# Values of stick-breaking attention by seven block products instead of eight

## The chip, the cores and the metric

The kernel runs on one core of a Trainium2 chip. The metric is the device time of one execution in microseconds (us), as the median of several runs. The engines that matter are TensorE (PE in the profile, with its weight loads as PEld), VectorE (DVE), ScalarE (ACT), GpSimd (POOL) and the queues of transfers that SyncE (SP) and GpSimd issue.

## The reference, cut to what matters

A trunk of two layers over 512 rows of 1024 columns, all in fp32. The first layer is gated linear attention and an MLP, the second stick-breaking attention and an MLP. What the change touches is this:

```python
h = layer_norm(ALPHA * h + mix, ...)                # mix: gated attention, ends with o @ w_o
h = layer_norm(ALPHA * h + sq_relu_mlp(h, w_up, w_down), ...)
kv = h @ kv_w                                       # 1024 x 2048
k_sh, v_sh = kv[..., :D], kv[..., D:]               # keys, values
q = h @ sb_w_q
# ... attention by blocks of 128 queries, then @ sb_w_o, layer_norm,
# and a second MLP with its layer_norm, whose result is the output
```

`sq_relu_mlp` is `relu(x @ w_up) ** 2 @ w_down`, with 4096 columns in between.

## The kernel before, in words

Every fp32 product is made of three matmuls. A number is split into `hi`, its rounding to the matrix engine's format fp32r, and `lo`, what is left; a product is hi by hi, hi by lo and lo by hi. For a tile of weights `split_tile` does it (L67): ScalarE copies to `hi` (L70), VectorE subtracts to `lo` (L72). For activations `put` does it (L97 to L99), out of PSUM or SBUF; tiles of split activations are named `T`. Weights come in tiles of 128 by 1024: `raw` for plain ones, with three buffers, and `B` for blocks that are added up. `hi` and `lo` have six buffers each.

The 512 rows are four row tiles, `hs[0]` to `hs[3]` (h300 to h303 in the profile's names). A row tile's work after a stage is: `add` (L163) of the two halves of 512 columns out of PSUM, statistics (L175 and L179 on VectorE, then `rs` on GpSimd, L184), `centre` (L188), `affine` by gain and bias (L194), and a turn: `turn_affine` (L219) transposes four 128 by 128 pieces on TensorE (L224), applies gain and bias to the columns on ScalarE (L227) and splits the result with `put`. So gain and bias are applied twice, once to the turned copy that the next product reads and once to the row tile that the residual needs. `finish` (L238) runs that for a stage's tiles and hands back the turns that it leaves to the next stage (`late`).

Two kinds of products exist. `rows` and its like multiply one row tile or column tile directly. `seven` (L274) multiplies a 512 by 1024 matrix by a 1024 by 1024 one as two by two blocks with seven block products in place of eight, after Strassen and Winograd. It needs sums and differences of blocks on both sides. A block product has 24 matmuls of 512 columns, two halves of 12 (`part`, L328). Sums of weights are made on VectorE, or, for the last call of a stage (`ends`), by accumulating transfers on GpSimd's queue (`more`, L286). `plain_b` (L312) is the one factor that is a plain block of weights. The kernel before uses `seven` for the output projection of gated attention and for the MLPs' way down. Each caller has a pool of its own for the blocks `B`.

The values (L741 to L747) are made by `rows`: for each half of 512 columns and each row tile 24 matmuls, 192 in all. The turns of row tiles 2 and 3 are done between them. ScalarE copies each result to SBUF (L745). Keys and queries of the first pair of heads follow.

In an MLP's last two groups of columns on the way up, ScalarE does both the relu and the square (L685 and L689); in the others VectorE multiplies (L687). At the very end `done1` gathers the statistics of each row tile, those of tiles 0 and 1 on ScalarE (`stats_apart`, L196), and `norm` (L208) applies mean, gain and bias on VectorE and stores.

A scheduler sets the order on each engine from the program's order and its own costs; an instruction that is wrapped in `keep_in_program_order` stays behind those that the program has ahead of it. Each engine runs its instructions in that order and waits on semaphores.

## Time and profile before

| | |
|---|---|
| median of 3 runs | 1141.9 us (1141.05 to 1141.96) |
| the profiled execution | 1141.15 us, its span 1139.4 us |
| TensorE busy | 1119.6 us (98%) |
| VectorE busy | 802.8 us (70%) |
| ScalarE busy | 559.3 us (49%) |
| GpSimd busy | 180.3 us (16%) |

A row of a timeline gives a start, a length, the engine, the line, and in square brackets the idle time before it with the engine, tile and line that ended it. A row of a group gives the count, the busy time, the mean length of one in ns, and the idle time before its instructions. Matmuls overlap, so a matmul's length is not its pace.

### The profile page before, as it was taken

To read this page: it belongs to the slowest core of one execution; us is meant where nothing else is said; L and a number is where in the kernel's file an instruction comes from. 1 tells how busy PE (TensorE), PEld (TensorE's weight loads), DVE (VectorE), ACT (ScalarE), POOL (GpSimd) and SP (SyncE) were. 2 spreads that over 40 slices of the span, in tenths; PEclk is the share of its full clock that TensorE was granted. 3 is DMA by queue.
4 is the path that set the end of the run, shared out by engine and by line. 5 is a ranking of instruction groups with operands and counts; after the bars stand their busy time and mean duration, and the time that the engine had idled before them with its cause. 6 is when DMAs were issued, how large, how long until landed. Compare 5 with 4: busy or idle time off the path is not lost.

```text
span 1139.4 us, 14091 instructions
## 1 busy us (share of the span) xinstructions
PE 1119.6 (98%) x5389; PEld 924.7 (81%) x5389; DVE 802.8 (70%) x972; ACT 559.3 (49%) x831; POOL 180.3 (16%) x225
## 2 busy tenths in 40 slices
PE   8999999999999999999999999999999999999996
PEld 7778887898888888887888877777988888888874
DVE  4576638977756846848946878787777767567478
ACT  4354436653533524636635666754545435336262
POOL 1010123020000100122302444340100000001221
PEclk9999999999999999999999999999999999999999
DMA  7441299493670770796344121211865816707871
GB/s 239 124 120 48 75 269 202 133 300 112 164 224 19 194 203 29 199 207 130 111 112 130 56 74 38 74 38 37 257 187 125 237 45 161 227 19 191 181 128 74
DMA packets 104936, 156.47 MB, mean 137 GB/s; under 512 B 12258, under 2 KB 37218, under 8 KB 104868
## 3 DMA queue, kind: packets, MB, share of 16 engines
q1 hardware_dynamic: 86916, 120.96, 33.1%
q0 software_dynamic: 17952, 34.61, 17.9%
q8 instruction: 42, 0.69, 0.2%
q14 instruction: 26, 0.21, 0.1%
HBM read 153.45 MB, written 2.10 MB: 137 GB/s over the span
## 4 chain that ended last, share of the span: by engine, by line
PE 80%; DVE 13%; ACT 3%; issue 2%; POOL 1%; DMA 0%; POOLq 0%; SPq 0%; DVEq 0%; ACTq 0%
PE ps L334 27%; PE ps L93 17%; PE ps L94 16%; PE ps L95 16%; DVE r L798 4%; DVE lo L72 3%; ACT wt L813 1%; DVE h L194 1%; DVE T L99 1%; DVE ps L790 1%; DVE h L168 1%; ACT hi L70 1%; DVE qs L773 1%; DVE bst L175 1%; POOL rs L184 1%
## 5 line engine op out<-in xcount | busy, mean ns | idle before, releaser
L334 PE MATMUL ps<-hi,T 128*128 128x512 f32 x1008 | 314.1, 390 | 3.7 <-ACT T L98 2.3
L93 PE MATMUL ps<-T,hi 128*128 128x512 f32 (+1 forms) x768 | 288.6, 376 | 0.0
L94 PE MATMUL ps<-T,hi 128*128 128x512 f32 (+1 forms) x768 | 285.8, 372 | 0.5 <-DVE T L99 0.4
L95 PE MATMUL ps<-T,lo 128*128 128x512 f32 (+1 forms) x768 | 285.4, 372 | 0.0
L72 DVE TENSOR_TENSOR lo<-raw,hi 128x1024 fp32r<-128x1024 f32 x134 | 163.8, 1226 | 136.5 <-ACT hi L70 136.1
L70 ACT ACTIVATE hi<-raw 128x1024 fp32r<-128x1024 f32 x134 | 142.7, 1068 | 198.7 <-PE ps L94 67.6
L334 PEld LDWEIGHTS ps<-hi,T 128*128 128x128 f32 x1008 | 189.1, 188 | 44.9 <-ACT T L98 4.1
L72 DVE TENSOR_TENSOR lo<-B,hi 128x1024 fp32r<-128x1024 f32 x108 | 131.1, 1223 | 93.3 <-ACT hi L70 93.1
L334 PE MATMUL ps<-lo,T 128*128 128x512 f32 x504 | 196.3, 389 | 0.0
L70 ACT ACTIVATE hi<-B 128x1024 fp32r<-128x1024 f32 x108 | 114.2, 1060 | 150.2 <-PE ps L94 103.6
L95 PEld LDWEIGHTS ps<-T,lo 128*128 128x128 f32 x768 | 144.7, 188 | 25.1
L94 PEld LDWEIGHTS ps<-T,hi 128*128 128x128 f32 x768 | 144.8, 189 | 24.6 <-DVE T L99 0.9
L93 PEld LDWEIGHTS ps<-T,hi 128*128 128x128 f32 x768 | 144.6, 188 | 24.5 <-issue 1.1
L288 POOL DMA_DIRECT2D B<-in_mlp_w_down_dram x52 | 62.5, 1231 | 539.8 <-DMA B<-in_mlp_w_down_dram 427.4
L334 PEld LDWEIGHTS ps<-lo,T 128*128 128x128 f32 x504 | 94.6, 188 | 19.4
L93 PE MATMUL ps<-hi,T 128*128 128x512 f32 x256 | 102.8, 402 | 0.0
L94 PE MATMUL ps<-lo,T 128*128 128x512 f32 x256 | 100.5, 393 | 0.0
L95 PE MATMUL ps<-hi,T 128*128 128x512 f32 x256 | 100.5, 393 | 0.0
L168 DVE TENSOR_TENSOR h<-h,ps 128x512 f32<-128x512 f32 x110 | 74.7, 681 | 7.0 <-PE ps L95 3.5
L798 DVE TENSOR_TENSOR_SCAN r<-r,begin 128x512 f32<-128x512 f32 x40 | 66.3, 1664 | 0.2
L799 POOL TENSOR_TENSOR w<-w,r 128x512 f32<-128x512 f32 x40 | 51.5, 1288 | 75.7 <-DVE r L798 60.4
L93 PEld LDWEIGHTS ps<-hi,T 128*128 128x128 f32 x256 | 48.6, 190 | 10.5 <-issue 1.3
(171 smaller groups left out, 1189.3 us busy)
## 6 DMA issues: line engine op xcount, KB each, us to landing
raw<-in_mlp_w_up_dram SPq DMA_DIRECT2D x64, 512.0 KB, 5.5
B<-in_mlp_w_down_dram SPq DMA_DIRECT2D x64, 512.0 KB, 4.9
B<-in_mlp_w_down_dram POOLq DMA_DIRECT2D x52, 512.0 KB, 7.9
raw<-in_gla_w_in_dram SPq DMA_DIRECT2D x20, 512.0 KB, 3.7
raw<-in_mlp_w_down_dram SPq DMA_DIRECT2D x16, 512.0 KB, 5.1
raw<-in_kv_w_dram SPq DMA_DIRECT2D x16, 512.0 KB, 3.8
B<-in_gla_w_o_dram POOLq DMA_DIRECT2D x14, 512.0 KB, 8.1
B<-in_gla_w_o_dram SPq DMA_DIRECT2D x8, 512.0 KB, 7.3
```

The costliest lines, as they stand in the source:

```text
L70: nc.scalar.activation(hi, raw, AF.Copy)
L72: nc.vector.tensor_tensor(lo, raw, hi.bitcast(F32), op=ALU.subtract)
L93: nc.tensor.matmul(ps, lhsT=a[0], rhs=b[0], start=first, stop=False)
L94: nc.tensor.matmul(ps, lhsT=a[0], rhs=b[1], start=False, stop=False)
L95: nc.tensor.matmul(ps, lhsT=a[1], rhs=b[0], start=False, stop=last)
L99: keep(nc.vector.tensor_tensor(lo, ps, hi.bitcast(F32), op=ALU.subtract))
L168: nc.vector.tensor_tensor(h, h, ps, op=op)
L175: nc.vector.bn_stats(out=self.st[:, n, :], in_=h)
L288: nc.gpsimd.dma_start(out=b.rearrange("p (a b) -> p a b", a=2), in_=weights(k, h, j), accum_op=ALU.add)
L334: nc.tensor.matmul(banks[s], lhsT=a(k, s)[x], rhs=b[k][y], start=opens and (k, x, y) == (0, 0, 0), stop=closes and (k, x, y) == (3, 1, 0), ...
L798: nc.vector.tensor_tensor_scan(down, down, begins[kind][:, ::-1], 1.0, op0=ALU.mult, op1=ALU.max)
L799: nc.gpsimd.tensor_tensor(w, w, r[:, 1:S + 1], op=ALU.mult)
```

## The change

Values are now made by `seven` too, 7 x 24 = 168 matmuls. The left factor is h as turned columns. Three of the seven products read blocks that are split already (q11, q12 and q22 of `h2T`). The others need sums of unsplit blocks of h; so an unsplit copy `hF` is kept: for row tiles 0 and 1 it is rebuilt as hi + lo, for tiles 2 and 3 the turn writes it. `Values.add` has ScalarE copy the first part of each result and VectorE add the rest.

The blocks `B` live in one pool from the output projection of gated attention to the values, and in a second one for the last MLP. In `plain_b` ScalarE's `hi` of plain weights keeps its place in the program, which is behind the splits of activations. In the MLPs' last two groups on the way up two of four squares go to VectorE. In the last stage the norms of row tiles 0 and 1 come with a later step, and a norm's first operation keeps its place.

```diff
@@ split_piece / split_tile
-        return split_tile(raw, a)
+        return split_tile(raw, a, **how)
...
+    def split_tile(raw, a, keep=lambda ins: ins):
...
-        nc.scalar.activation(hi, raw, AF.Copy)
+        keep(nc.scalar.activation(hi, raw, AF.Copy))
@@ norm
-                nc.vector.scalar_tensor_tensor(h, h, self.less, g, op0=ALU.add, op1=ALU.mult)
+                first = nc.vector.scalar_tensor_tensor(h, h, self.less, g, op0=ALU.add, op1=ALU.mult)
...
+            tc.keep_in_program_order(first)
@@ seven
-    def seven(a1, a2, weights, pool, hs, fresh, norms=(), mid=None, ends=False):
+    def seven(a1, a2, weights, pool, hs, fresh, norms=(), mid=None, ends=False,
+              split=None, sums=None):
...
-                hi, lo = split_piece(weights(k, h, j), 2)
+                hi, lo = split_piece(weights(k, h, j), 2, keep=tc.keep_in_program_order)
...
+        sums = sums or unit(F32)
+        s1, s2 = sums[:, :, lo_t], sums[:, :, hi_t]
+        if split:
+            ws = [None, None]
+            q11, q12, q22 = ((lambda k, s, u=u, c=c: split.k(4 * u + k, c + 128 * s, 128))
+                             for u, c in ((0, 0), (1, 0), (1, 256)))
+            product(q11, split_b(2), ys, True, False, 0, 0)
+            second = q12, split_b(3), xs, True, True
+            for b22, b12, b11, b21 in bs:
+                tt(b11, b22, b11, op=ALU.add)
+                tt(b21, b21, b11, op=ALU.add)
+            for s in range(2):
+                mid(s)
+                part(s, *second)
+                add(s, xs, 0, 0)
+            product(q22, split_b(3), ws, True, True, 1, 0)
+            tt(s1, a22, a21, op=ALU.subtract)
+            third = split_a(s1), split_b(1)
+            minus(s2, s1, a11)
+            product(*third, zs, True, False, 1, 1)
+            fourth = split_a(s2), split_b(2)
+            minus(a12, a12, s2)
+            product(*fourth, ys, False, False, 0, 1)
+            product(split_a(a12), plain_b(1, 1), zs, False, True, 0, 1)
+            tt(a21, a11, a21, op=ALU.subtract)
+            p7 = split_a(a21), split_b(0)
+            for s in range(2):
+                part(s, *p7, ys, False, True)
+                add(s, ys, 1, 1)
+                add(s, ys, 1, 0)
+            return
@@ output projection of the gated attention, mlp
+    bx = tc.tile_pool(name="blocks", bufs=1, reuse_waits="tile")
+    bp = bx.__enter__()
...
-    steps = seven(*onT, lambda k, h, j: block(gla_w_o[0], 512 * k + 256 * h, 512 * j), opp, hs, True, norms=range(NT),
+    steps = seven(*onT, lambda k, h, j: block(gla_w_o[0], 512 * k + 256 * h, 512 * j), bp, hs, True, norms=range(NT),
...
-                if g < NG - 2:
+                if g < NG - 2 or f % 2:
...
-            return seven(*sq[g:g + 2], lambda k, h, j: block(mlp_w_down[l], 512 * (g + k) + 256 * h, 512 * j), mlp_,
-                         hs, g == 0, **how)
+            return seven(*sq[g:g + 2], lambda k, h, j: block(mlp_w_down[l], 512 * (g + k) + 256 * h, 512 * j), bp, hs,
+                         g == 0, **how)
@@ values
+    vs = [unit(F32), unit(F32)]
+    class Values:
...
+        def add(self, n, ps, first, last, op):
+            v = vs[n][:, self.t, :]
+            if first:
+                nc.scalar.activation(v, ps, AF.Copy, scale=1.0 if op == ALU.add else -1.0)
+            else:
+                nc.vector.tensor_tensor(v, v, ps, op=op)
+    hF = [vp.tile([P, 4, 512], F32, name=f"hF{u}") for u in range(2)]
+    def turn_late(i):
+        late[i](lambda u, t: hF[u][:, :, 128 * t:128 * t + 128])
+        if i == 0:
+            for u in range(2):
+                c = slice(0, 256)
+                nc.vector.tensor_tensor(hF[u][:, :, c], h2T.hi[u][:, :, c].bitcast(F32),
+                                        h2T.lo[u][:, :, c].bitcast(F32), op=ALU.add)
+    for _ in seven(*hF, lambda k, h, j: block(kv_w, 512 * k + 256 * h, D + 512 * j), bp, [Values(t) for t in range(NT)],
+                   True, mid=turn_late, split=h2T, sums=vp.tile([P, 4, 512], F32, name="sums")):
+        pass
...
-    for n in range(2):
-        pcs = pieces_512(kv_w, 0, 8, D + 512 * n)
-        for t in range(NT):
-            nc.scalar.activation(vs[n][:, t, :], rows(h2T, t, pcs, K8), AF.Copy)
-            if late:
-                late.pop(0)(chain)
@@ done1
         for t in steps:
             if t < 0:
-                continue
-            if t < 2:
-                hs[t].stats_apart(lambda: work(4))
+                norm(~t)
+            elif t < 2:
+                hs[t].stats_apart(whole())
             else:
                 hs[t].stats()
-            cuts = (0, 1024) if t < NT - 1 else (0, 512, 768, 1024)
-            hs[t].norm(vec, lambda c: store(t, c), [slice(*c) for c in zip(cuts, cuts[1:])])
+        norm(2)
+        norm(3)
```

How the rows move at three places. VectorE, in the stage of the values, from the centring of the last row tiles on. T is a split of activations, lo a split of weights, h300 to h303 are the row tiles (their last number differs between the kernels). Before:

```order
L72 TENSOR_TENSOR lo800_4743<-raw798_4739,hi799_4741 128x1024
L179 BN_AGGR mv769_4536<-bst761_4475 128x2
L72 TENSOR_TENSOR lo803_4749<-raw801_4745,hi802_4747 128x1024
L182 TENSOR_SCALAR ve770_4538<-mv769_4536 128x1
L194 TENSOR_TENSOR h300_1602<-h300_1602,lng816_4869 128x512
L188 TENSOR_SCALAR h303_1605<-h303_1605,mv769_4536,rs771_4540 128x1024
L99 TENSOR_TENSOR T691_4144<-w787_4613,T690_4143 128x4x128
L194 TENSOR_TENSOR h300_1602<-h300_1602,lng816_4869 128x512
L194 TENSOR_TENSOR h300_1602<-h300_1602,lnb817_4870 128x512
L99 TENSOR_TENSOR T693_4146<-w789_4625,T692_4145 128x4x128
L194 TENSOR_TENSOR h300_1602<-h300_1602,lnb817_4870 128x512
```

Now, from the same place to the splits for the third product (B is a block of weights, hF the unsplit copy of h, T682 the values):

```order
L359 TENSOR_TENSOR B776_4564<-B774_4558,B776_4564 128x1024
L359 TENSOR_TENSOR B780_4574<-B778_4568,B780_4574 128x1024
L360 TENSOR_TENSOR B777_4566<-B777_4566,B776_4564 128x1024
L360 TENSOR_TENSOR B781_4576<-B781_4576,B780_4574 128x1024
L99 TENSOR_TENSOR T691_4150<-hF0_4555,T690_4149 128x4x128
L99 TENSOR_TENSOR T693_4152<-hF1_4556,T692_4151 128x4x128
L781 TENSOR_TENSOR hF0_4555<-T690_4149,T691_4150 128x4x256
L781 TENSOR_TENSOR hF1_4556<-T692_4151,T693_4152 128x4x256
L772 TENSOR_TENSOR T772_4553<-T772_4553,ps794_4650 128x512
L99 TENSOR_TENSOR T691_4150<-hF0_4555,T690_4149 128x4x128
L99 TENSOR_TENSOR T693_4152<-hF1_4556,T692_4151 128x4x128
```

The `affine` rows (lng, lnb) have moved behind the stage's sums; four sums of blocks, two rebuilt halves and the adds of results stand in their place, and the two splits of the third product's weights come two rows after the last one shown.

ScalarE, at the third product of the last way down of the first MLP. Before:

```order
L98 ACTIVATE T717_4223<-s2620_3703 128x4x256
L70 ACTIVATE hi728_4278<-B698_4157 128x1024
L70 ACTIVATE hi730_4282<-B702_4167 128x1024
L70 ACTIVATE hi736_4352<-raw735_4350 128x1024
L98 ACTIVATE T718_4228<-T704_4171 128x4x256
L98 ACTIVATE T727_4275<-T704_4171 128x4x256
```

Now:

```order
L98 ACTIVATE T717_4229<-s2620_3709 128x4x256
L70 ACTIVATE hi728_4284<-B698_4163 128x1024
L70 ACTIVATE hi730_4288<-B702_4173 128x1024
L98 ACTIVATE T718_4234<-T704_4177 128x4x256
L98 ACTIVATE T727_4281<-T704_4177 128x4x256
L98 ACTIVATE T734_4353<-s2689_4140 128x4x256
L70 ACTIVATE hi736_4358<-raw735_4356 128x1024
L70 ACTIVATE hi739_4364<-raw738_4362 128x1024
```

The copy of plain weights (raw) stood ahead of two splits of activations (T<-T) and now stands behind three.

VectorE, at the end of the program, when the last product of the last MLP runs. Before:

```order
L212 SCALAR_TENSOR_TENSOR h300_1602<-h300_1602,s21511_9076,lng1457_8833 128x1024
L204 TENSOR_SCALAR s21512_9098<-s21512_9098 128x1
L212 SCALAR_TENSOR_TENSOR h301_1603<-h301_1603,s21512_9098,lng1457_8833 128x1024
L216 SCALAR_TENSOR_TENSOR h300_1602<-h300_1602,s21511_9076,lnb1458_8834 128x1024
L216 SCALAR_TENSOR_TENSOR h301_1603<-h301_1603,s21512_9098,lnb1458_8834 128x1024
L175 BN_STATS bst1513_9120<-h302_1604 128x6
L168 TENSOR_TENSOR h303_1605<-h303_1605,ps1474_8883 128x512
L168 TENSOR_TENSOR h302_1604<-h302_1604,ps1473_8869 128x512
L175 BN_STATS bst1514_9135<-h303_1605 128x6
```

Now:

```order
L203 TENSOR_SCALAR s21525_9128<-s21525_9128 128x1
L211 SCALAR_TENSOR_TENSOR h300_1609<-h300_1609,s21525_9128,lng1471_8885 128x1024
L203 TENSOR_SCALAR s21526_9147<-s21526_9147 128x1
L168 TENSOR_TENSOR h303_1612<-h303_1612,ps1488_8935 128x512
L216 SCALAR_TENSOR_TENSOR h300_1609<-h300_1609,s21525_9128,lnb1472_8886 128x1024
L175 BN_STATS bst1528_9184<-h303_1612 128x6
L211 SCALAR_TENSOR_TENSOR h301_1610<-h301_1610,s21526_9147,lng1471_8885 128x1024
L168 TENSOR_TENSOR h302_1611<-h302_1611,ps1487_8921 128x512
L216 SCALAR_TENSOR_TENSOR h301_1610<-h301_1610,s21526_9147,lnb1472_8886 128x1024
L175 BN_STATS bst1527_9166<-h302_1611 128x6
```

Both norms of tiles 0 and 1 stood ahead of the add of tile 3. Now the add of tile 3 stands behind the first operation of tile 0's norm.

More of the change, by code (lines that the diff above doesn't have):

```diff
@@ L194, in affine, with stats_apart @@
                     nc.vector.tensor_tensor(self.h[:, c], self.h[:, c], v[:, c], op=op)
-        def stats_apart(self, work):
-            room = work()
+        def stats_apart(self, room):
             junk = room[:, 0:D]
@@ L668, in four, with room @@
             return mlp_.tile([P, 4, 512], F32, tag="s2", bufs=3, name=nm("s2"))
-        def work(n=1):
-            return four()[:, 0:n, :].rearrange("p a b -> p (a b)")
+        def room(u, t):
+            return blocks4(four()[:, 0, :])
         def up(g):
@@ L679, in up @@
                     if g == 0 and c0 == f == 0 and (k == 5 or k == 4 and len(late) > 1):
-                        late.pop(0)(work)
+                        late.pop(0)(room)
                     mm3(pss[f][:, c0:c0 + cn], tuple(w[:, 128 * f:128 * f + 128] for w in pcs[k]),
@@ L705, in mlp @@
         steps = down(NG - 2, norms=range(NT) if l == 0 else (2, 3), ends=True)
-        got = done(steps, work)
+        got = done(steps, room if l == 0 else lambda: four().rearrange("p a b -> p (a b)"))
         ml.__exit__(None, None, None)
@@ L710, in yoco_kernel, with done0, __init__ @@
     h2T = Split(0)
-    def done0(steps, work):
+    def done0(steps, room):
         h2T.grow()
         h2T.grow()
-        return finish(steps, lncols(0, 1), hs, h2T, work)
-    late = mlp(0, hT, late, vec, done0)
+        return finish(steps, lncols(0, 1), hs, h2T, room)
+    late = mlp(0, hT, late, vec, done0, bp)
+    vx = tc.tile_pool(name="values", bufs=1, reuse_waits="tile")
+    vp = vx.__enter__()
+    vs = [unit(F32), unit(F32)]
+    class Values:
+        def __init__(self, t):
+            self.t = t
+        def add(self, n, ps, first, last, op):
[15 more added lines that the diff above has]
+        pass
+    vx.__exit__(None, None, None)
+    bx.__exit__(None, None, None)
+    gl.__exit__(None, None, None)
     sbx = tc.tile_pool(name="sb", bufs=1, reuse_waits="tile")
@@ L871, in part2, with done1 @@
             hs[t].add(n, pss[n], False, True)
-    late = finish(by_tiles(part2), vcols, hs, h3T, chain)
+    late = finish(by_tiles(part2), vcols, hs, h3T, lambda u, t: blocks4(chain()))
     sbx.__exit__(None, None, None)
-    def done1(steps, work):
+    def done1(steps, whole):
         vec = lnvec(1, 1)
@@ L880, in store, with norm @@
             nc.sync.dma_start(out=out2[128 * t:128 * t + 128, c], in_=hs[t].h[:, c])
+        def norm(t):
+            cuts = (0, 1024) if t < NT - 1 else (0, 512, 768, 1024)
+            hs[t].norm(vec, lambda c: store(t, c), [slice(*c) for c in zip(cuts, cuts[1:])])
         for t in steps:
             if t < 0:
-                continue
-            if t < 2:
-                hs[t].stats_apart(lambda: work(4))
+                norm(~t)
+            elif t < 2:
+                hs[t].stats_apart(whole())
             else:
                 hs[t].stats()
-            cuts = (0, 1024) if t < NT - 1 else (0, 512, 768, 1024)
-            hs[t].norm(vec, lambda c: store(t, c), [slice(*c) for c in zip(cuts, cuts[1:])])
-    mlp(1, h3T, late, vec, done1)
+        norm(2)
+        norm(3)
+    bx = tc.tile_pool(name="blocks2", bufs=1, reuse_waits="tile")
+    mlp(1, h3T, late, vec, done1, bx.__enter__())
+    bx.__exit__(None, None, None)
 _INS = ['x', 'gla_w_in', 'gla_w_a2', 'gla_b_a', 'gla_norm_g', 'gla_w_o', 'kv_w', 'sb_w_q', 'sb_w_o',
```

26 lines of the change are left out of this document (13 added, 13 removed).

## The prediction

> **What bounds the kernel now.** I read the page's first part, then its groups, then the chain of waits, then TensorE's rows one by one.
>
> ```profile
> span 1139.4 us, 14091 instructions
> PE 1119.6 (98%) x5389; PEld 924.7 (81%) x5389; DVE 802.8 (70%) x972; ACT 559.3 (49%) x831; POOL 180.3 (16%) x225
> ...
> L334 PE MATMUL ps<-hi,T 128*128 128x512 f32 x1008 | 314.1, 390 | 3.7 <-ACT T L98 2.3
> ...
> L72 DVE TENSOR_TENSOR lo<-B,hi 128x1024 fp32r<-128x1024 f32 x108 | 131.1, 1223 | 93.3 <-ACT hi L70 93.1
> ```
>
> TensorE has work in 98% of the span, so a matmul less is time less, as long as its operands are there. A matmul's 390 ns are latency; its pace stands in the chain of waits:
>
> ```profile
> 292.24 38.08 PE ps L334 x168
> ...
> 562.11 0.87 PE ps L224 x8
> ```
>
> 38.08 / 168 = 0.2267 us. One block product has 24 matmuls, 5.44 us; eight transposes of a row tile (L224) take 0.87. The stretch that the change rewrites, and the few places where TensorE waits, in its timeline:
>
> ```profile
> 237.15 0.39 PE L94 MATMUL ps<-T,hi 128*128 128x256 f32 x1 [0.37 <-DVE T L99]
> 526.90 0.50 PE L334 MATMUL ps<-hi,T 128*128 128x512 f32 x1 [0.74 <-ACT T L98]
> 550.67 0.39 PE L334 MATMUL ps<-lo,T 128*128 128x512 f32 x1
> 551.21 1.09 PE L224 MATMUL ps<-ident,h 128*128 128x128 f32 x8
> 556.50 0.39 PE L93 MATMUL ps<-hi,T 128*128 128x512 f32 x1
> 601.81 0.39 PE L93 MATMUL ps<-T,hi 128*128 128x512 f32 x1
> 749.52 0.55 PE L808 MATMUL ps<-ident,w 128*128 128x128 f32 x3 [1.65 <-POOL w L799]
> 1100.72 0.50 PE L334 MATMUL ps<-hi,T 128*128 128x512 f32 x1 [0.74 <-ACT T L98]
> 1126.99 0.50 PE L334 MATMUL ps<-hi,T 128*128 128x512 f32 x1 [1.44 <-DVE h L168]
> ```
>
> The values begin at 556.50 and the keys of the first pair at 601.81. What the other engines do in between, by windows (columns: the stretch, then busy time of PE, PEld, DVE, ACT and POOL):
>
> ```profile
> 556.50:579.00 22.50, 22.50 (x109) 18.81 (x108) 21.26 (x35) 15.56 (x31) 6.78 (x13) 1.00 0.41 113
> 579.00:601.81 22.81, 22.81 (x102) 18.88 (x101) 6.14 (x7) 7.50 (x9) 0.00 (x0) 1.00 0.43 125
> 601.81:621.00 19.19, 19.19 (x91) 16.16 (x90) 9.56 (x12) 8.67 (x12) 2.77 (x3) 1.00 0.55 160
> ```
>
> TensorE never pauses there. VectorE is busy for 21.26 of 22.50 us first, for 6.14 of 22.81 us afterwards: its work sits in the first half of the stage, and this decides the case.
>
> **The values: TensorE's side.** 192 matmuls become 168: 24 x 0.2267 = 5.44 us less. Nothing else on TensorE grows; the transposes of row tiles 2 and 3 stay 16 in number.
>
> **The values: VectorE's side.** The old stage asked eight splits of plain weights of VectorE, and filled its room with the 16 halves of `affine` (L194). The new one asks fourteen splits (twelve of blocks), four block sums, two rebuilt halves of h, four sums of h, five splits of activations of 1024 columns and eight adds. The rows that price them, grouped by shape, then the timeline's runs, which give the pace back to back:
>
> ```profile
> L99 DVE TENSOR_TENSOR T<-T,T 128x1024 fp32r<-128x1024 f32 x23 | 28.0, 1219 | 1.2 <-ACT T L98 1.2
> L194 DVE TENSOR_TENSOR h<-h,lng 128x512 f32<-128x512 f32 x24 | 15.8, 685 | 0.0
> L369 DVE TENSOR_TENSOR B<-B,B 128x1024 f32<-128x1024 f32 x12 | 14.7, 1222 | 0.2
> ...
> 569.48 1.29 DVE L194 TENSOR_TENSOR h<-h,lng 128x512 f32<-128x512 f32 x2
> 577.91 3.49 DVE L72 TENSOR_TENSOR lo<-raw,hi 128x1024 fp32r<-128x1024 f32 x3
> ```
>
> 1024 columns take (3.49 - 1.22) / 2 = 1.13 us each in a row, 512 columns 1.29 - 0.69 = 0.60. All the kinds above last alike (1219, 1222, 1223 ns), so the new ones are priced so too.
>
> When does VectorE get to the third product (q22 by b21)? In its order these stand ahead of that product's weights: the centring of the last row tile (L188), four block sums, two splits of 512, the two rebuilt halves, an add, two splits of 512, an add, and the two `lo` themselves. The centring waits for a chain through GpSimd:
>
> ```profile
> 549.50 1.86 ACT L227 ACTIVATE s<-ps,bcol,gcol 128x128 f32<-128x128 f32 x5 [0.69 <-PE ps L224]
> ...
> 557.51 0.71 ACT L98 ACTIVATE T<-s 128x512 fp32r<-128x512 f32 x1
> ...
> 565.74 0.81 DVE L188 TENSOR_SCALAR h<-h,mv,rs 128x1024 f32<-128x1024 f32 x1 [1.24 <-POOL rs L184]
> ...
> 548.90 1.41 POOL rs L184
> ```
>
> The columns of row tiles 0 and 1 now start on ScalarE about 1.2 us later (their transposes stand seven matmuls into the last product, 7 x 0.2267 less what they used to wait), and one weight split of about 0.95 us fewer stands between them: they end near 558.5. VectorE's last split of them ends at 559.1, statistics and one weight split follow, and after GpSimd's 1.41 us the centring of tile 3 starts at 562.2 to 563.1; I take 562.8. From there: 0.73 + 4 x 1.13 + 2 x 0.60 + 2 x 1.13 + 0.60 + 2 x 0.60 + 0.60 + 1.13 = 12.24, so the first `lo` is ready at 575.05 and the second 1.13 later.
>
> And TensorE? The stage starts at 556.50 - 0.74 - 0.15 = 555.6 (the wait at 526.90 goes, below; 551.21 less 550.67 and 0.39 is the 0.15, which goes with the transposes' new place). Two products (10.9), 16 transposes (1.7) and a wait of 0.4 for tile 2 bring it to 568.6. It issues one matmul of product three and then waits for `lo` until 575.05: **6.2 us idle, more than the 5.44 saved.** On from there: product three ends at 575.05 + 23 x 0.2267 = 580.3. VectorE does a sum, two `lo` and a split by 580.7; product four needs that split at its third matmul, 580.75, just in time, and ends at 585.7. A sum, two `lo`, two sums and a split end at 587.5; product five wants that split at 586.2 and waits 1.3. Six and seven have theirs: 592.5, 597.9, 603.4. The keys start 603.4 - 601.81 = **1.6 later** than now, with the gain of 0.89 at the start already inside. Ends: with a centring at 562.2 it is 1.0; if VectorE never held TensorE, 601.81 - 0.89 - 5.44 = 595.5, a gain of 6.3; I take 1.6, since VectorE's queue is in order and each item has its row.
>
> **What spills.** Twelve of 16 `affine` halves leave the stage and now stand between weight splits of keys and queries: 12 x 0.60 = 7.2 us in 598 to 621, where VectorE has 9.56 of 19.19 busy. There is cover for it, so 0; without it up to 3 (a rival below).
>
> **ScalarE, plain weights after activations.** In each block multiply `hi<-raw` now stands behind the splits of activations. At the third product of the last one it held them up:
>
> ```profile
> 516.20 1.23 DVE L72 TENSOR_TENSOR lo<-B,hi 128x1024 fp32r<-128x1024 f32 x1 [4.23 <-ACT hi L70]
> 524.84 1.07 ACT L70 ACTIVATE hi<-raw 128x1024 fp32r<-128x1024 f32 x1 [3.02 <-PE ps L334]
> 525.81 1.99 ACT L98 ACTIVATE T<-T 128x1024 fp32r<-128x1024 f32 x2
> ```
>
> The split that TensorE waits for at 526.90 could start up to a microsecond sooner. VectorE's sum ahead of it (L348) now stands ahead of a split of 1024 too, so it is not late: both waits of 0.74 go, **-0.74** at 1100.72 (the twin at 526.90 is in the 1.6). The plain weights behind them are used two products, 10.9 us, later: 0. By the same regrouping at 237.15 **-0.37**. Bounds of the three: 0 and -1.1.
>
> **Squares.** Eight go from ScalarE to VectorE (0.60 each). In two of four per group they run in pauses such as the 4.23 us ahead of 516.20; the last stands behind one `lo`, +0.6 on a split that has 2 us until its product. 0; uncovered, 0.6 twice.
>
> **Blocks that keep their place.** Loads move earlier on SP's queue, and four accumulating loads on GpSimd's stand ahead of an `rs` of 1.41 us. If one waits for its block, centring and transposes behind it wait too: 0 to +2. TensorE shows no wait on a load after its first microseconds, so nothing is to be gained; I take 0.
>
> **The end.** VectorE's last rows:
>
> ```profile
> 1123.27 2.48 DVE L216 SCALAR_TENSOR_TENSOR h<-h,s,lnb 128x1024 f32<-128x1024 f32 x2
> 1125.66 0.69 DVE L175 BATCH_NORM_STATS2 bst<-h 128x6 f32<-128x512 f32 x1
> 1126.26 1.27 DVE L168 TENSOR_TENSOR h<-h,ps 128x512 f32<-128x512 f32 x2
> ...
> 1130.27 0.68 DVE L168 TENSOR_TENSOR h<-h,ps 128x512 f32<-128x512 f32 x1
> ...
> 1134.81 1.54 DVE L216 SCALAR_TENSOR_TENSOR h<-h,rs,lnb 128x512 f32<-128x512 f32 x3 [0.44 <-POOL rs L184]
> ```
>
> Four products of gain and bias stood ahead of the add at 1126.26 that frees TensorE's bank. Now one stands ahead: the add comes near 1123, the wait of 1.44 goes and TensorE ends 1.44 sooner. VectorE does not: from the last add (1129.4 by my count) it still has statistics of both tiles (1.2 us) and three operations of 1.2 ahead of the last pieces, so these start at 1134.2 instead of 1134.81: **-0.6**. Ends: -1.44 and +0.5 (the store of tile 2 leaves a microsecond later and shares the DMA engines with the last pieces).
>
> **Sum.** 1.6 - 0.74 - 0.37 - 0.6 = -0.1 against the profiled 1141.15. The median, 1141.9, lies 0.75 above it, so the forecast is 1141.8. What a measurement of this kernel can tell from no change is 0.2%, 2.3 us: 1139.6 to 1144.2 is "same".
>
> **The rivals.**
>
> *VectorE keeps up.* The centring starts earlier, or the sums run while TensorE is in product two. For it: the second window leaves VectorE 16.7 us free (22.81 - 6.14), so only the order within the stage is in the way. Against it: four sums of blocks stand in front of the item that TensorE needs next. With no wait at all the stage gains 6.3: 1141.9 - 6.3 - 1.7 = 1133.9; with half of the waits (7.5 / 2 = 3.7 less) 1138.0. Chance 0.32.
>
> *Spill into attention.* Slower. Place: the first pair's keys, 601 to 621. 9.56 us of VectorE's work plus 7.2 of `affine` plus four adds of 0.60 is 19.2 in 19.19 us: full. As soon as the `lo` of a query weight stands behind six halves (3.6 us) with no slack left, TensorE waits: +3, 1144.8. It decides once VectorE's queue enters that stretch more than about 2 us late. Chance 0.18.
>
> *TensorE comes back slow after a wait of 6 us.* No row shows such a thing: the longest pause in mid-program is the 1.65 at 749.52, and the windows' clock column reads 1.00. If half a product (12 matmuls) ran at half pace, 12 x 0.2267 = 2.7 more, less product five's wait of 1.3, which it absorbs: +1.4; a whole product, +4.1: 1143.2 to 1145.9. Chance 0.08.
>
> [...]
>
> **Chances.** Forecast 0.42, keeping up 0.32, the two slower ones 0.26 together. The likeliest one's own range is 1139.6 to 1144.2; 8 times in 10 reaches well into the first rival and just past the second's price: 1135.5 to 1145.5. Faster 0.32, same 0.42, slower 0.26.
>
> **What would show it.** Right: TensorE waits 5 to 7 us for a `lo` of VectorE at the third product of the values and 1 to 1.5 at the fifth, keys start at 603 to 604, VectorE has no idle microsecond between 563 and 596, no wait at 526.9, 1100.7 and 1127. Wrong: keys start before 600 (VectorE was not the bound), a longer stretch from keys to the first weights (the spill), or a clock column under 1.00 behind the wait.

## The result and the profile after

The change makes the kernel slower.

| | before | after |
|---|---|---|
| median | 1141.6 us (1141.05 to 1141.96, 4 runs) | 1157.8 us (1157.0 to 1159.1, 4 runs) |
| ratio | | 1.0144 (95% interval 1.0126 to 1.0161) |
| span of the profiled execution | 1139.4 us | 1155.8 us |

The page of the changed kernel begins with its span and TensorE's busy time:

```profile
span 1155.8 us, 14086 instructions
PE 1118.4 (97%) x5365; PEld 924.0 (80%) x5365; DVE 836.5 (72%) x1008; ACT 558.8 (48%) x833; POOL 182.2 (16%) x229
```

TensorE is busy 1.2 us less and the span is 16.4 longer: the time is in waits. The rows of TensorE's timeline with the longest ones, and the first matmul of the keys:

```profile
222.24 1.94 PE L224 MATMUL ps<-ident,h 128*128 128x128 f32 x8 [6.79 <-DVE ve L182]
563.95 1.97 PE L224 MATMUL ps<-ident,h 128*128 128x128 f32 x8 [6.92 <-DVE ve L182]
585.57 1.02 PE L340 MATMUL ps<-hi,T 128*128 128x512 f32 x2 [1.59 <-ACT hi L70]
590.48 0.79 PE L340 MATMUL ps<-lo,T 128*128 128x512 f32 x1 [3.89 <-DVE lo L72]
619.06 0.39 PE L93 MATMUL ps<-T,hi 128*128 128x512 f32 x1
```

Two waits of nearly 7 us stand at transposes of row tile 0, at the end of gated attention and at the end of the first MLP. The third and fourth row are one wait, at the third product of the values: 1.59 ahead of its first two matmuls and 3.89 ahead of the next, 5.5 together.

What these waits leave behind stands in the windows, whose third column from the end is the clock that TensorE was granted:

```profile
215.00:222.00 7.00, 0.45 (x2) 0.03 (x1) 5.38 (x11) 1.93 (x3) 2.99 (x3) 0.76 0.97 303
222.00:226.00 4.00, 3.76 (x19) 3.49 (x20) 3.53 (x7) 2.63 (x8) 0.56 (x1) 0.57 1.08 229
230.00:240.00 10.00, 10.00 (x83) 9.81 (x82) 9.40 (x16) 6.54 (x13) 1.93 (x2) 1.00 0.49 162
564.00:568.00 4.00, 4.00 (x21) 3.61 (x22) 3.56 (x5) 4.00 (x10) 0.55 (x1) 0.66 1.08 195
590.00:594.00 4.00, 3.52 (x8) 2.81 (x9) 4.00 (x5) 1.82 (x2) 0.00 (x0) 0.50 0.00 0
594.00:598.00 4.00, 4.00 (x19) 3.26 (x18) 4.00 (x4) 1.15 (x2) 0.00 (x0) 0.99 0.00 0
```

Behind each of the three waits TensorE runs about 4 us at 0.5 to 0.66 of its clock. Eight transposes took 1.09 us before (551.21) and take 1.94 and 1.97 here.

Marks of both profiles tell where the 16.4 us came in:

| mark | before | after | later by |
|---|---|---|---|
| second product of gated attention's projection waits (L334, now L340) | 193.47 | 193.35 | -0.12 |
| first whole way down without a pause | 292.24 | 299.66 | 7.42 |
| keys of the first pair | 601.81 | 619.06 | 17.25 |
| last matmul | 1129.63 | 1143.94 | 14.31 |
| VectorE's last pieces | 1134.81 | 1151.41 | 16.60 |

The stretch with the first wait and its slow clock lost 7.5 us, the stretch to the keys another 9.8. What TensorE gains later is given back at the end.

**The first wait** begins with a load. GpSimd's rows of the changed kernel (accumulating loads, and `rs`), then ScalarE and VectorE:

```profile
196.39 1.69 POOL L294 DMA_DIRECT2D B<-in_mlp_w_down_dram  x1
200.44 1.19 POOL L294 DMA_DIRECT2D B<-in_gla_w_o_dram  x1 [2.36 <-DMA B<-in_gla_w_o_dram]
201.17 1.69 POOL L294 DMA_DIRECT2D B<-in_mlp_w_down_dram  x1
219.44 1.20 POOL L294 DMA_DIRECT2D B<-in_mlp_w_down_dram  x1 [0.20 <-issue]
220.19 1.05 POOL L184 TENSOR_TENSOR rs<-ve,mhalf 128x1 f32<-128x1 f32 x1
...
213.03 1.06 ACT L70 ACTIVATE hi<-B 128x1024 fp32r<-128x1024 f32 x1 [7.58 <-DMA B<-in_gla_w_o_dram]
...
214.13 1.22 DVE L72 TENSOR_TENSOR lo<-B,hi 128x1024 fp32r<-128x1024 f32 x1 [5.42 <-ACT hi L70]
215.27 1.28 DVE L168 TENSOR_TENSOR h<-h,ps 128x512 f32<-128x512 f32 x2
221.28 0.81 DVE L188 TENSOR_SCALAR h<-h,mv,rs 128x1024 f32<-128x1024 f32 x1 [1.61 <-POOL rs L184]
```

The last part of w_o's block is issued at 200.44 and has landed only when `hi` starts, at 213.03. VectorE's `lo` waits for `hi`, the adds of row tiles 0 and 1 stand behind that `lo`, their statistics behind the adds, and only then comes `rs`, which in addition stands behind a load (1.2 us). Before, the same part went out here, and the same `hi` waited for TensorE alone:

```profile
197.92 1.20 POOL L288 DMA_DIRECT2D B<-in_gla_w_o_dram  x1 [1.32 <-DMA B<-in_gla_w_o_dram]
...
204.71 1.06 ACT L70 ACTIVATE hi<-B 128x1024 fp32r<-128x1024 f32 x1 [0.29 <-PE ps L334]
```

**The second wait** has another cause. Here the statistics are ready, and `rs` stands behind loads that wait themselves (SyncE's queue of plain loads, then GpSimd, then VectorE):

```profile
547.48 6.88 SPq L300 DMA_DIRECT2D B<-in_kv_w_dram  x4
...
559.88 1.19 POOL L294 DMA_DIRECT2D B<-in_kv_w_dram  x1 [13.41 <-DMA B<-in_kv_w_dram]
562.00 1.04 POOL L184 TENSOR_TENSOR rs<-ve,mhalf 128x1 f32<-128x1 f32 x1
...
554.97 0.14 DVE L182 TENSOR_SCALAR ve<-mv 128x1 f32<-128x1 f32 x1
563.08 0.81 DVE L188 TENSOR_SCALAR h<-h,mv,rs 128x1024 f32<-128x1024 f32 x1 [7.29 <-POOL rs L184]
```

`ve` is ready at 555.1, `rs` starts at 562.0: an accumulating load waits 13.4 us for the plain load that it adds to, and `rs` waits with it. That plain load was held until 547.48, behind a wait for a `lo` of the MLP, and then took about 12 us to land.

### The profile page after: what moved, and what is told of

Read it like the earlier page. It is cut to its first block, busy times and chain, and to the rows that moved or that the text cites. A ratio compares the mean times of both kernels' runs of the same rounds, so it can differ in the third digit from the quotient of the medians.

```text
span 1155.8 us, 14086 instructions
## 1 busy us (share of the span) xinstructions
PE 1118.4 (97%) x5365; PEld 924.0 (80%) x5365; DVE 836.5 (72%) x1008; ACT 558.8 (48%) x833; POOL 182.2 (16%) x229
## 4 chain that ended last, share of the span: by engine, by line
PE 73%; DVE 14%; DMA 4%; issue 3%; ACT 3%; POOL 2%; SPq 0%; DVEq 0%; POOLq 0%; ACTq 0%
PE ps L340 27%; PE ps L93 15%; PE ps L94 14%; PE ps L95 14%; DVE r L860 4%; DMA B<-in_gla_w_o_dram 3%; DVE lo L72 3%; ACT wt L875 1%; DVE T L99 1%; DMA B<-in_kv_w_dram 1%; POOL B L294 1%; DVE qs L835 1%; DVE h L194 1%; DVE ps L852 1%; ACT hi L70 1%
## 5 line engine op out<-in xcount | busy, mean ns | idle before, releaser
L340 PE MATMUL ps<-hi,T 128*128 128x512 f32 x1120 | 350.4, 392 | 2.4 <-ACT hi L70 1.6
L340 PEld LDWEIGHTS ps<-hi,T 128*128 128x128 f32 x1120 | 211.2, 189 | 47.6 <-ACT hi L70 2.0
L72 DVE TENSOR_TENSOR lo<-raw,hi 128x1024 fp32r<-128x1024 f32 x128 | 156.6, 1228 | 103.9 <-ACT hi L70 103.6
L340 PE MATMUL ps<-lo,T 128*128 128x512 f32 x560 | 219.5, 392 | 3.9 <-DVE lo L72 3.9
L70 ACT ACTIVATE hi<-raw 128x1024 fp32r<-128x1024 f32 x128 | 134.7, 1064 | 156.6 <-DMA raw<-in_mlp_w_up_dram 60.3
L72 DVE TENSOR_TENSOR lo<-B,hi 128x1024 fp32r<-128x1024 f32 x120 | 145.2, 1219 | 86.4 <-ACT hi L70 86.2
L70 ACT ACTIVATE hi<-B 128x1024 fp32r<-128x1024 f32 x120 | 124.5, 1056 | 156.1 <-PE ps L94 105.4
L340 PEld LDWEIGHTS ps<-lo,T 128*128 128x128 f32 x560 | 105.8, 189 | 26.0 <-DVE lo L72 4.2
L93 PE MATMUL ps<-hi,T 128*128 128x512 f32 x192 | 77.7, 406 | 0.0
L95 PE MATMUL ps<-hi,T 128*128 128x512 f32 x192 | 75.4, 392 | 0.0
L98 ACT ACTIVATE T<-s 128x1024 fp32r<-128x1024 f32 (+1 forms) x50 | 47.9, 973 | 34.5 <-DVE s L726 14.1
## 6 DMA issues: line engine op xcount, KB each, us to landing
B<-in_gla_w_o_dram POOLq DMA_DIRECT2D x14, 512.0 KB, 10.4
```

What stands on the lines that cost most here:

```text
L70: keep(nc.scalar.activation(hi, raw, AF.Copy))
L72: nc.vector.tensor_tensor(lo, raw, hi.bitcast(F32), op=ALU.subtract)
L93: nc.tensor.matmul(ps, lhsT=a[0], rhs=b[0], start=first, stop=False)
L95: nc.tensor.matmul(ps, lhsT=a[1], rhs=b[0], start=False, stop=last)
L98: keep(nc.scalar.activation(hi, ps, AF.Copy))
L340: nc.tensor.matmul(banks[s], lhsT=a(k, s)[x], rhs=b[k][y], start=opens and (k, x, y) == (0, 0, 0), stop=closes and (k, x, y) == (3, 1, 0), ...
```

## The experiments

Each ran beside the kernel before, whose median over all of them was 1141.7 us.

**A pool of its own for each caller.** In all three calls of `seven`:

```diff
-    ... block(gla_w_o[0], ...), bp, hs, True, ...
+    ... block(gla_w_o[0], ...), opp, hs, True, ...
-    return seven(*sq[g:g + 2], ..., bp, hs, ...)
+    return seven(*sq[g:g + 2], ..., mlp_, hs, ...)
-    for _ in seven(*hF, ..., bp, [Values(t) ...
+    for _ in seven(*hF, ..., vp, [Values(t) ...
```

> The changed kernel with one edit undone: each caller of seven keeps a pool of its own for the blocks B (gated attention's, the MLPs', and the values' own one). Queue theory: in the changed kernel GpSimd's rs of a row tile stands behind accumulating loads of the next stage's blocks, at the end of gated attention and at the end of the first MLP; TensorE waits 6.8 and 6.9 us there and then runs about 4 us at a clock of 0.57 to 0.66, about 16.5 us together. With own pools these loads come after the rs, so 1141 to 1142. Values theory: the time was lost in the values' stage itself (VectorE-bound, plus its slow clock); then no more than 3 us come back, 1155 or more.

Measured: 1154.2 us, ratio 1.0114 (1.0098 to 1.0130). Neither number of the two theories. The waits at both transposes are gone (0.42 is the longest at any transposes), but now the values' blocks are late, since their pool opens only when the MLP's closes:

```profile
558.29 0.88 PE L340 MATMUL ps<-hi,T 128*128 128x512 f32 x2 [3.57 <-ACT hi L70]
566.35 0.80 PE L340 MATMUL ps<-lo,T 128*128 128x512 f32 x1 [7.18 <-DVE lo L72]
```

So the shared pool causes both waits, and without it the values in seven products wait for their weights instead.

**All accumulating loads in program order.** The shared pool stays:

```diff
-            nc.gpsimd.dma_start(out=b..., in_=weights(k, h, j), accum_op=ALU.add)
+            tc.keep_in_program_order(nc.gpsimd.dma_start(out=b..., in_=weights(k, h, j), accum_op=ALU.add))
```

> The changed kernel with its shared pool, but the accumulating loads on GpSimd keep their place in the program, which is behind the rs of the stage before. The plain loads of the blocks on SP's queue stay as early as in the changed kernel. Queue theory: the order on GpSimd alone is the cause, so 1141 to 1142.5, and both waits at the transposes (6.8 and 6.9) are under 0.5. Traffic theory (a rival): the early plain loads crowd the DMA engines, whose share is 1.0 in those stretches, and hold the stage's end whatever GpSimd's order is; then the waits stay above 3 us each and the time above 1149.

Measured: 1195.4 us, ratio 1.0472 (1.0452 to 1.0492), a failed experiment: it also held back the loads that finish a stage's own blocks.

```profile
225.47 1.06 ACT L70 ACTIVATE hi<-B 128x1024 fp32r<-128x1024 f32 x1 [14.50 <-DMA B<-in_gla_w_o_dram]
...
233.09 1.94 PE L224 MATMUL ps<-ident,h 128*128 128x128 f32 x8 [10.98 <-DVE ve L182]
```

It does not decide between the theories. It shows the chain of the first wait once more: `hi` of w_o's last block waits for its load, and the transposes behind it wait too.

**The shared pool alone, in the kernel before.** The pools of the diff, with nothing else of the change (with them goes what makes room for them: the tile `cs` gets a pool that closes early, and gated attention's pool closes later). Here one of the calls:

```diff
-    ... block(gla_w_o[0], ...), opp, hs, True, ...
+    ... block(gla_w_o[0], ...), bp, hs, True, ...
```

> The kernel before with one edit done: blocks in one pool across stages. By its order four accumulating loads stand ahead of the rs at the end of gated attention, none ahead of those at the end of the first MLP (there the values take plain weights). Queue theory: one wait of about 6.8 with its slow clock, so 1141.6 + 7.4 to 8.5 = 1149 to 1150. Values theory: 1141.6, since the values are the old ones.

Measured: 1150.3 us, ratio 1.0081 (1.0064 to 1.0098), 0.3 above the expected 1149 to 1150, by the expected way. There is one wait at the transposes, and none at the end of the MLP:

```profile
221.86 1.94 PE L224 MATMUL ps<-ident,h 128*128 128x128 f32 x8 [7.39 <-DVE ve L182]
```

The pool alone costs 8.7 us.

**All but the values.** Of the changed kernel the values are undone.

```diff
-    for _ in seven(*hF, ...)
+    for n in range(2):
+        pcs = pieces_512(kv_w, 0, 8, D + 512 * n)
+        for t in range(NT):
+            nc.scalar.activation(vs[n][:, t, :], rows(h2T, t, pcs, K8), AF.Copy)
...
```

> The changed kernel with the old values (eight products, plain weights, 192 matmuls) and all other edits, the shared pool among them. Queue theory: the first wait stays (+7.4), the second is gone with the values' accumulating loads, the two waits of 0.74 and 0.37 in the old kernel stay away: 1141.6 + 7.4 - 1.9 = 1147.1, 1146 to 1148.5. Values theory (all of the loss is in the values' stage): 1140.

Measured: 1149.3 us, ratio 1.0072 (1.0057 to 1.0087), 0.8 above the upper end. The second wait is gone with the values' blocks. With the run before, it puts about half of the loss on each end.

**Only the opening loads in program order.** This separates what the first wait is made of:

```diff
-                    more(b, h, *other)
+                    more(b, h, *other, keep=tc.keep_in_program_order)
```

> The changed kernel, shared pool and all, but only those accumulating loads that open a block multiply keep their place, behind the rs of the stage before (in the run that kept all of them those that close one were late too). Two theories for the two waits of the changed kernel. Queue theory for both: both waits gone, 1141 to 1142. Traffic at the first, queue at the second: at the end of gated attention the last accumulated block of w_o lands late among the early loads (12.6 us after its issue instead of under 8), and that does not need GpSimd's order, only the early plain loads on SP's queue, so a wait of 4 to 7 stays at the first place; at the end of the first MLP the wait of 6.9 with its slow clock goes. Then 1149 to 1150. In both the values' accumulated blocks arrive later, which can lengthen the wait at the values' third product.

Measured: 1152.3 us, ratio 1.0100 (1.0084 to 1.0116).

```profile
216.78 1.07 PE L224 MATMUL ps<-ident,h 128*128 128x128 f32 x8 [1.26 <-DVE ve L182]
565.17 1.09 PE L224 MATMUL ps<-ident,h 128*128 128x128 f32 x8 [1.33 <-DVE ve L182]
576.66 1.32 PE L340 MATMUL ps<-hi,T 128*128 128x512 f32 x2 [4.00 <-ACT hi L70]
584.39 0.79 PE L340 MATMUL ps<-lo,T 128*128 128x512 f32 x1 [6.42 <-DVE lo L72]
```

Both waits shrink to 1.3. For the first this is less than the traffic theory said (4 to 7), although the plain loads on SP's queue are as early as in the changed kernel: the early accumulating loads on GpSimd's queue were the larger part. Of the 11 us of waits that this saves 5 came back at the third product, 10.4 us instead of 5.5, as the expectation allowed. How long w_o's accumulating loads took to land between 195 and 216 (transfers by group; the last column is the median in us) in the kernel before, in this one, and in the changed one:

```profile
B<-in_gla_w_o_dram POOLq DMA_DIRECT2D x2, 512.0 KB, 6.1
```

```profile
B<-in_gla_w_o_dram POOLq DMA_DIRECT2D x2, 512.0 KB, 8.6
```

```profile
B<-in_gla_w_o_dram POOLq DMA_DIRECT2D x2, 512.0 KB, 10.6
```

The last one decides. It landed 6.3, 8.5 and 12.5 us after its issue, and with the early plain loads it was issued 2.6 us later too, so `hi` started at 204.71, 209.15 and 213.03. The first 4.4 us of delay, which the plain loads alone cause, left a wait of 1.26: most of it was covered. The 3.9 us that the MLP's accumulating loads add were not covered, and `rs` came 1.2 behind a load and took 0.5 longer: 1.26 + 3.9 + 1.2 + 0.5 = 6.9, against the 6.79 of the row.

**The first MLP's opening loads alone.**

```diff
+                    more(b, h, *other, **({} if split else dict(keep=tc.keep_in_program_order)))
```

> The changed kernel, where the accumulating loads that open a block multiply keep their place except those of the values. This tells the two waits apart. If each has its own cause, the first (6.8 at the end of gated attention) shrinks to about 1.3, as in e5_keep_opening, and the second (6.9 at the end of the first MLP) stays; the values' blocks are as early as in the changed kernel, so the third product's wait stays 5.5. Then 1157.8 - 5.5 - 1.4 = 1150.9, 1149.5 to 1152. If the second wait hung on the first, it goes too: under 1145.

Measured: 1154.3 us, ratio 1.0115 (1.0099 to 1.0130), above the range. In its trace the first wait shrinks to 1.58, as expected, and the third product waits 1.61 and 3.88, as in the changed kernel. The second wait stays, but shorter:

```profile
558.21 1.97 PE L224 MATMUL ps<-ident,h 128*128 128x128 f32 x8 [4.85 <-DVE ve L182]
```

Those 2.1 us are not won: the clock behind it stays low for longer (0.50 from 558 to 562 and 0.76 from 562 to 566, against 0.66 and 1.00 in the changed kernel from 564 to 572). From the first whole way down (295.98) to the keys (615.43) 319.45 us pass, against 319.40 in the changed kernel. The first 193 us, the same program, took 2.1 longer in the profiled execution (195.50 for the row that stands at 193.35), which hides part of the gain there; whether they did in the other executions is not known. The second wait does not hang on the first.

**The orders alone.** Old values, a pool for each caller; what stays are the splits on ScalarE, the squares and the norms.

> The changed kernel with the old values and with a pool for each caller: what is left of the change is the order of splits on ScalarE, the four squares, and the norms at the end. By the steps on record for these alone: -0.74 twice, -0.37, -0.6 at the end, so 1141.6 - 2.4 = 1139.2 (1138.5 to 1140.5). If the squares or the norms cost what the other edits gain: 1141.6.

Measured: 1142.1 us, ratio 1.0006 (0.9997 to 1.0016): no gain. The waits at 526.90, 1100.72 and 1126.99 are gone, and in their place stand

```profile
559.55 0.50 PE L94 MATMUL ps<-lo,T 128*128 128x512 f32 x1 [0.86 <-DVE lo L72]
...
1127.64 0.39 PE L340 MATMUL ps<-hi,T 128*128 128x512 f32 x1
```

a wait for the old values' first weights, whose split is now behind others, and at the end TensorE's last matmul at 1127.64, 2.0 sooner than before, with VectorE's last pieces at 1135.12, 0.3 later.

**The same with the old norms.**

```diff
-            tc.keep_in_program_order(first)
...
-                norm(~t)
+                continue
...
-        norm(2)
-        norm(3)
+            norm(t)
```

> The kernel of e6_orders_only with the old order of norms at the end. In e6_orders_only TensorE ends 2.0 us sooner but VectorE's last operation starts 0.3 later. With the old norms TensorE waits 1.44 again and ends later, and VectorE's end follows it at the old distance (5.2 us): 1142.1 - 0.9 = 1141.2. If the new norms were worth what the step on record says (-0.6): 1142.7.

Measured: 1143.0 us, ratio 1.0010 (1.0001 to 1.0020). By the medians the new norms are worth 0.9 us, nearer the step on record than what I had meanwhile thought; but the intervals of the two kernels' ratios overlap, so the times alone do not show it. The profiles show the way: the old norms cost a wait of 2.44 here, the clock falls behind it, and VectorE's last pieces start at 1137.00 instead of 1135.12:

```profile
1127.80 0.77 PE L339 MATMUL ps<-hi,T 128*128 128x512 f32 x1 [2.44 <-DVE h L168]
...
1127.70:1130.00 2.30, 2.20 (x5) 1.80 (x6) 2.23 (x7) 0.00 (x0) 0.00 (x0) 0.54 0.73 296
```

**ScalarE's order alone, in the kernel before.**

```diff
-                hi, lo = split_piece(weights(k, h, j), 2)
+                hi, lo = split_piece(weights(k, h, j), 2, keep=tc.keep_in_program_order)
```

> The kernel before with one edit: ScalarE's plain weights behind the splits of activations in each block multiply. By the step on record the two waits of 0.74 go, and nothing else moves: 1141.5 - 1.5 = 1140.0 (1139.8 to 1141). If the waits come back elsewhere, as a split of the values' weights that is late: 1141.5.

Measured: 1142.3 us, ratio 1.0005 (0.9996 to 1.0015). Both waits of 0.74 went from their places. In their stead stand a new wait at the values' first weights and a longer one at the end (1.91 instead of 1.44), with a slow clock behind it that is shown in the last section:

```profile
559.82 0.50 PE L94 MATMUL ps<-lo,T 128*128 128x512 f32 x1 [0.60 <-DVE lo L72]
1127.31 0.50 PE L334 MATMUL ps<-hi,T 128*128 128x512 f32 x1 [1.91 <-DVE h L168]
```

**The shared pool later.** Opening loads kept, and the pool opened after gated attention's projection, which has its own again.

> The kernel of e5_keep_opening, with the shared pool opened only after gated attention's output projection, which gets its own pool back. Then no block of the MLP is loaded while w_o's blocks are on their way. Traffic theory: the first wait is gone too, 7 to 8 us less than e5_keep_opening. What is left of the change is then the values in seven products, with VectorE's wait of 5 to 6 and a slow clock behind it, against 5.4 saved: 1140 to 1143, unless the accumulated blocks of the values, now issued behind the last rs, come late; then up to 10 more. Queue theory alone: as e5_keep_opening.

Measured: 1153.3 us (1149.2 to 1157.0), ratio 1.0105 (1.0070 to 1.0139). The first wait is gone (the longest there is 0.40), as the traffic theory says, but the 7 to 8 us that it promised did not come. At the third product the blocks come late again (3.96 and 6.37), and at 552.50 the last way down of the MLP now waits 3.57 us. The four times lie far apart (two near 1150, two near 1157), and the profile is of an execution of 1157.0.

**An attempt at a better kernel.** Blocks of the values loaded right behind the first two `rs` of the last way down, rebuilt halves later, sums of one half on GpSimd.

```diff
+                if t == 2:
+                    kvb.extend(load_blocks(kvw, bp, keep=tc.keep_in_program_order))
...
+                tt2 = (lambda *a, **o: tc.keep_in_program_order(nc.gpsimd.tensor_tensor(*a, **o))) if h else tt
-                tt(b11, b22, b11, op=ALU.add)
+                tt2(b11, b22, b11, op=ALU.add)
```

> An attempt at the better kernel. As e7_pool_later, and the values' blocks are loaded right behind the first two rs of the last block multiply, so that neither those rs nor the blocks wait for each other; the two rebuilt halves of h keep their place behind the third product's weights; the block sums of one half run on GpSimd. VectorE's work between the last centring and the third product's weights shrinks by 2 x 1.13 + 2 x 1.13 = 4.5 of 12.3 us, so the wait there falls from 5.5 to about 1 to 2 and no slow clock follows: 1139.2 (e6_orders_only) - 5.4 + 2 + 1 = 1136.8, 1135 to 1139. If loads of the blocks or GpSimd's sums come late instead: over 1141.

Measured: 1150.0 us, ratio 1.0079 (1.0057 to 1.0101). That is far above the expected 1135 to 1139. The third product still waits 2.31 and 4.36. VectorE, and GpSimd beside it:

```profile
563.91 2.89 DVE L188 TENSOR_SCALAR h<-h,mv,rs 128x1024 f32<-128x1024 f32 x1 [0.44 <-POOL rs L184]
566.72 3.40 DVE L364 TENSOR_TENSOR B<-B,B 128x1024 f32<-128x1024 f32 x1
...
563.85 5.19 POOL L363 TENSOR_TENSOR B<-B,B 128x1024 f32<-128x1024 f32 x2
```

While GpSimd adds, VectorE's centring takes 2.89 us instead of 0.8 and its block sum 3.40 instead of 1.2: of the 4.5 us moved away, 4.3 came back. Two halves of `affine` and a sum of h, another 2.3 us, also came to stand ahead of the third product's `lo`, so its wait is longer than in the changed kernel.

**The same with all sums on VectorE.** The first sum of h now keeps its place behind the third product's weights, too.

> As e8_reordered_values, but all block sums on VectorE again, and the rebuilt halves and the sums of h keep their place behind the third product's weights. Theory of the shared path: in e8_reordered_values a centring took 2.89 us and a block sum 3.40 while GpSimd added blocks; without that they take 0.8 and 1.2 again. Theory of VectorE as the bound of the stage: work that is only moved behind the third product's weights comes back as a wait at the fourth or fifth product, so the third product's wait falls from 5.5 to 3 or 4 but the stage ends no earlier than 2 us behind that of e6_orders_only: 1144 to 1147. If order alone were in the way: 1139.

Measured: 1146.5 us, ratio 1.0042 (1.0025 to 1.0059), inside the range of the second theory, though not by its way, since no wait stands at the fourth or fifth product. The durations are back:

```profile
569.84 0.81 DVE L188 TENSOR_SCALAR h<-h,mv,rs 128x1024 f32<-128x1024 f32 x1 [0.45 <-POOL rs L184]
570.57 2.36 DVE L364 TENSOR_TENSOR B<-B,B 128x1024 f32<-128x1024 f32 x2
```

The third product waits 1.62 and 1.54. It is the best of the kernels with the values in seven products, and 4.9 us slower than before. Another 4.34 us are lost at 552.79, where the last way down waits for a row tile. The start of that is a block of the MLP that lands late, as at the first wait, now beside the values' early plain loads:

```profile
547.28 2.01 ACT L70 ACTIVATE hi<-B 128x1024 fp32r<-128x1024 f32 x2 [7.30 <-DMA B<-in_mlp_w_down_dram]
```

The profile is of an execution of 1149.5 us, and two of the other three took 1145.4, so not all of these waits need stand behind the median. No version beat the kernel before.

## Why the prediction was wrong

**Blocks that keep their place: the step that failed.** It took 0, with +2 as the upper end. It cost two waits of 6.8 and 6.9 us with a slow clock behind each: 8.7 us where only the pool was changed; the kernel with all but the values lies 8.5 below the changed one, and most of that is the second wait. Undoing the pool, or holding back the opening loads alone, took both waits away or down to 1.3. The step saw that four accumulating loads stand ahead of an `rs`, and priced the row that it had, the `rs` of 1.41. What counts is how long the loads ahead of it wait, 13.4 us at the second place, for a plain load that itself went out late and took about 12 us. And from "TensorE shows no wait on a load" it took only that nothing was to be gained, and did not ask what could be lost. A row such as that of `hi<-B` at 204.71 says only that the load had landed by then, not how long before: it was half a microsecond (197.92 + 6.3 = 204.2). Loads that are issued 42 us earlier (the first at 183.6 instead of 225.7) compete with the one that is due (12.5 us from issue to landing instead of 6.3), and VectorE's queue passes the delay on to adds that need no weights: they start at 215.27, behind the `lo` of 214.13.

**The clock.** This was a rival at 0.08, priced for the third product only. The half pace in its price was my assumption; no row of the kernel before shows one. In the changed kernel it came true there (4 us at 0.50, about 2.0 us lost) and at both other waits (4 us at 0.57 and at 0.66). How long TensorE stays slow is not one figure here: behind the third product's wait the clock reads 0.50 from 590 to 594 and 0.99 from 594 on, but in the run with the first MLP's loads alone it took about 6 us behind a wait of 4.85 (0.50 for 4 us, then 0.76 for 4). Nor did it need a wait of 6 us: in the kernel with the old norms 0.54 was read behind one of 2.44.

**The values.** Here the price of VectorE's queue held, and the total by luck. From the last centring (578.07) to TensorE's first use of `lo` (590.48) 12.4 us passed; the step said 12.24 to the first `lo`.

```profile
578.07 0.82 DVE L188 TENSOR_SCALAR h<-h,mv,rs 128x1024 f32<-128x1024 f32 x1 [0.44 <-POOL rs L184]
589.21 2.35 DVE L72 TENSOR_TENSOR lo<-B,hi 128x1024 fp32r<-128x1024 f32 x2
```

The wait was forecast as 6.2 and is 5.5; that at the fifth product (1.3) does not show, absorbed by the slow pace, as the rival said. These 2.0 us less and the 2.0 that the slow clock costs, which the sum had at nothing, cancel. Taking the second wait (6.92 less the 0.15 of before) and its slow clock (4 x 0.34 = 1.4) from the 9.8 us that this stretch lost, 1.7 are left, against 1.6 forecast. That VectorE sets the third product's wait is shown by its rows, which leave no pause from 578.07 to that `lo`, and by the last attempt: with the two rebuilt halves (2.3 us) moved behind the `lo` the wait fell by 2.3, from 5.5 to 3.2. Whether an order exists in which VectorE keeps up is not shown. The spill into attention did not come: from the keys to the first whole way down behind attention the changed kernel took 264.15 us (883.21 - 619.06) and the one before 264.25.

**ScalarE's order.** Forecast -0.74 twice and -0.37. Each wait went from its place, but in the kernels with old values 0.6 to 0.9 stand at the values' first weights instead, the transposes' new place waits 0.42, and with the old norms the wait at the end grew from 1.44 to 1.91. Alone the edit is worth nothing (1.0005). The step asked only who is served sooner; who is served later on VectorE was left out.

**The end.** Forecast -0.6; the medians of the two kernels that differ in it are 0.9 apart, which is not clear of noise. The wait of 1.44 went and VectorE gave most of it back, as the step said; beside the kernel before, no gain is left (TensorE ends 2.0 sooner, VectorE's last pieces start 0.3 later).

**Squares.** No run separates them, so the 0 is untested; nothing in the profiles speaks against it.

## What to carry to other kernels

Before loads are let out of a pool earlier, find for each queue that they enter what stands behind them, and price it by what the load itself waits for, not by the length of the instruction behind it. Loads that come sooner can also slow those that are due, here from 6.3 us to 8.5 and 12.5: look for the block with the least slack and follow who waits behind its split. A saving on the busiest engine is worth nothing where another engine must do more than the saved time in the same stage: here 5.4 us were saved on TensorE, and it waited 5.5 us behind VectorE.

## What the runs showed that I had not expected

- TensorE's clock fell behind pauses shorter than the wait of 6 us that the rival was priced for: behind 1.91 us it was 0.82 and then 0.50, behind 2.44 us 0.54, behind 4.34 us 0.50, while in the kernel before, behind 1.44 (1126.99) and 1.65 (749.52), it stayed at 1.00. The rows of the kernel with ScalarE's order alone, and of the last attempt:

```profile
1127.30:1129.00 1.70, 1.69 (x6) 1.42 (x7) 1.70 (x3) 0.00 (x0) 0.00 (x0) 0.82 0.92 374
1129.00:1131.50 2.50, 2.50 (x7) 1.69 (x6) 1.61 (x4) 0.00 (x0) 1.45 (x1) 0.50 0.00 0
```

```profile
552.70:555.00 2.30, 2.21 (x5) 1.82 (x6) 2.15 (x6) 2.30 (x3) 1.08 (x2) 0.50 0.03 12
```

- An addition of 128 x 1024 on GpSimd (2.6 us each) slowed VectorE's operations beside it from 0.8 and 1.2 us to 2.9 and 3.4.
- The same first 193 us of a program took 2.1 us longer in one profiled execution than in another (195.50 against 193.35).
